# A decoder-layer kernel on one core: edits to the order of five stretches (first loads, a decay row, a state scaling, memory's weights, an output projection)

## The chip, the cores and the metric

The kernel runs on one core of a Trainium2 chip. The time is device microseconds of a whole execution. Before the change three runs took 1079.46, 1080.54 and 1083.1 us; their median is 1080.54. The engines are TensorE (PE; its weight loads are PEld), VectorE (DVE), ScalarE (ACT), GpSimd (POOL) and SyncE (SP, which here only issues loads and stores).

## What is computed

One step of one layer of a hybrid decoder, for a prompt of 512 tokens and 8 samples of 8 tokens, which share the weights (576 columns in all, width 1024). Each part stands between two RMS norms:

```python
proj = rms(x) * g_pre_mix @ w_in                    # z, xbc, dt, q, k, v, gates
y_ssd = ssd_scan(silu(conv(xbc)), dt, a, h_ssm)     # Mamba-2, 16 heads of 64, state 128
y_ssd = rms((y_ssd + d_skip * xs) * silu(z)) * g
h_ml  = rms(mlstm_scan(q, k, v, ig, logf, ...)) * g * sigmoid(og)
x = x + rms(concat(y_ssd, h_ml) @ w_out) * g_post_mix
mk, mv = u_mem @ w_mem_k, u_mem @ w_mem_v           # u_mem = rms(mem) * g_mem
x = x + rms(attention(rms(x) @ w_xq, mk, mv) @ w_xo) * g_post_x
x = x + rms((silu(u @ w_gate) * (u @ w_up)) @ w_down) * g_post_ffn
```

Results are both outputs, the new memory keys and values, and the new SSM, convolution and mLSTM states of both groups.

## The kernel before

Activations lie with the features on the 128 partitions, 8 tiles of 128 by 576 columns, in a handful of large slots (`SL`, numbered) that successive stages take over. The columns are worked in halves of 256 and 320 (288 and 288 from the cross-attention on). The matmuls are in fp32 accuracy by splitting: every operand is a rounded part (`whi`, `uh`, ...) and a rest (`wlo`, `ul`, ...), and each product is three matmuls, L208 (`uh` by `whi`), L209 (`ul` by `whi`) and L211 (`uh` by `wlo`). A weight tile of 128x1024 is therefore loaded by SyncE into `raw` (L181, two buffers), cast by ScalarE into `whi` (L186, three buffers), and subtracted by VectorE into `wlo` (L193); some of the rests come by L190 and L191, ScalarE and an adding load of GpSimd's. PSUM has three pools of banks; `pg`, of three banks, holds the projections' sums, which the other engines empty.

The stages follow one another: a start with warm-up matmuls on zeros (L309, NWARM of them) while the first loads land, the input projection with the scans between its tiles, the output projection (`out1`, `out2`), the memory's keys and values, the cross-attention with its output projection (`xo`), and the FFN. A scheduler sets the order in which each engine's instructions stand, by a model of their times. `tc.issue_after(i)` tells it to place an instruction after `i`; it is an order of placing and adds no wait between engines by itself.

The places that the change touches:

- Start. SyncE first loads `par` (L310, all gains and small parameters, 128x150), then the first pieces of two weight tiles (`raws`, L319 and L322) alternating with pieces of x (`xraw`, L320); two loads stand on ScalarE's queue. `uh` (L332) and `ul` (L333) scale x by a gain out of `par`; VectorE casts the first weights (L329). The first real matmuls are L349 to L351.
- Decay rows, up to 85 us. VectorE computes `sx` (L560, L561) and `gpr` (L563), ScalarE copies both into a row tile `r` (L565, L566), TensorE transposes `r` (`ps_ct`, L587), ScalarE copies the result into `CT` (L589), and the broadcast `ps_en` (L595) reads that. `d1t` (L578) is a rest of another row that VectorE computes for the stacked rows `cumst` and `sxst`.
- Mask products. For each head the SSD scan forms a mask (VectorE L670, ScalarE's exponential L672, the product `lm` with `cbs` L673) which `ps_yi` (L678) multiplies. The products are kept in the list `mults`, eight for each of two groups. Between them GpSimd scales the samples' states by their decay (L789, 128x1024, two for each of four b) after TensorE has read them (`ps_hs`, L781); for b = 2 the source places the scaling after `mults[7]`.
- z, from 245 us. VectorE multiplies z's bank by `rxb` (L1053) to begin its evacuation.
- Memory. `memraw` (slot 1) receives the memory's rows (L1234); four weight tiles of its keys and values go through `raw` like the output projection's own and are split into `wmh` and `wml` (L197, L198). Later slot 1 takes `x` again (L1261, L1262).
- `xo`. Eight tiles; each ends with a square for the norm (L270, L274) and an evacuation into `f_xo` (L1540), both on ScalarE. The first three tiles leave out their last two k until the attention's last head is done.

## Time and profile before

| | |
|---|---|
| median of three runs | 1080.54 us |
| profiled execution | 1079.74 us, span 1078.0 us, granted clock 0.999 |
| loads and stores | 182.02 MB, mean 169 GB/s |
| costliest group of TensorE | L208 of the input projection, 544 matmuls, 161.6 us, 297 ns each |
| costliest group of ScalarE | L186, 104 casts, 105.2 us, 1014 ns each |
| costliest group of VectorE | L193, 96 subtractions, 94.1 us, 982 ns each |

How to read the rows: a row of the timeline has the start and the duration in us, the engine, the line, the operation, output<-inputs with buffer numbers left out, the shapes, and how many instructions of the same kind the row holds; in brackets the idle time of the engine ahead of it and what ended that. An engine name with a q is its queue of load issues. A row of the waits has the waiting instruction, what it waited for, the sum in us, the number of times and the longest. A row of the stretches has the stretch, its length, TensorE's busy time with its number of matmuls, the granted clock as a share of full speed, the share of the load engines in use and GB/s.

### The profile page before, as it was taken

What the parts mean: (1) busy time and instruction counts of PE and PEld (TensorE: products, weight loads), DVE (VectorE), ACT (ScalarE), POOL (GpSimd) and SP (SyncE); (2) the same over time, 40 slices, a digit from 0 to 9 for tenths busy, and PEclk for the clock granted to TensorE, in tenths of its full rate; (3) what the DMA queues carried; (4) which work ended last, traced back from release to release, by engine and by line L of the source; (5) the groups of instructions that cost most, each with busy time, mean ns of one, the idle gap of its engine ahead of it and who ended that gap; (6) DMA issues with size and microseconds to landing.
All of it is one profiled execution on the core that took longest, in us unless ns stands there. A gap on an engine that the chain in (4) does not pass through costs nothing.

```text
span 1078.0 us, 20698 instructions
## 1 busy us (share of the span) xinstructions
PE 1068.0 (99%) x8124; PEld 1014.8 (94%) x8124; DVE 752.0 (70%) x1508; ACT 608.1 (56%) x1094; POOL 231.0 (21%) x304
## 2 busy tenths in 40 slices
PE   9999999999999999999999999999999999999997
PEld 9999887778999999999999989999999999999997
DVE  6897775658877775569755546766467887787556
ACT  7867522345654555556555445645567566656653
POOL 1444643313113121000154301100011111111000
PEclk9999999999999999999999999999999999999999
DMA  6786544426654438753468775743477697578532
GB/s 208 179 168 131 157 126 175 149 71 185 190 154 144 113 113 320 233 205 105 150 202 282 277 253 179 240 131 95 135 165 155 153 203 165 118 186 186 131 132 89
DMA packets 58822, 182.02 MB, mean 169 GB/s; under 512 B 6588, under 2 KB 11836, under 8 KB 58212
## 3 DMA queue, kind: packets, MB, share of 16 engines
q1 hardware_dynamic: 42740, 138.06, 39.2%
q0 software_dynamic: 15408, 41.69, 19.9%
q8 instruction: 64, 1.05, 0.4%
q10 hardware_dynamic: 576, 0.95, 0.3%
q14 instruction: 34, 0.28, 0.1%
HBM read 160.01 MB, written 20.65 MB: 168 GB/s over the span
## 4 chain that ended last, share of the span: by engine, by line
PE 95%; DVE 2%; DMA 2%; ACT 1%; issue 0%; SPq 0%; DVEq 0%; ACTq 0%
PE ps_in L208 6%; PE ps_in L211 6%; PE ps_in L209 6%; PE ps_v L850 5%; PE ps_o L211 3%; PE ps_g L1885 3%; PE ps_u L1885 3%; PE ps_g L1884 3%; PE ps_o L209 3%; PE ps_u L1886 3%; PE ps_g L1886 3%; PE ps_o L208 3%; PE ps_u L1884 3%; PE ps_dn L1884 2%; PE ps_dn L1885 2%; PE ps_dn L208 2%
## 5 line engine op out<-in xcount | busy, mean ns | idle before, releaser
L208 PE MATMUL ps_in<-uh,whi 128*128 128x320 f32 (+1 forms) x544 | 161.6, 297 | 0.3 <-ACT la L448 0.3
L211 PE MATMUL ps_in<-uh,wlo 128*128 128x320 f32 (+1 forms) x544 | 161.6, 298 | 0.0
L209 PE MATMUL ps_in<-ul,whi 128*128 128x320 f32 (+1 forms) x544 | 161.2, 296 | 0.0
L186 ACT CAST whi<-raw 128x1024 fp32r<-128x1024 f32 (+1 forms) x104 | 105.2, 1014 | 98.8 <-PE ps_in L209 25.7
L193 DVE TENSOR_TENSOR wlo<-raw,whi 128x512 fp32r<-128x512 f32 (+1 forms) x96 | 94.1, 982 | 68.7 <-ACT whi L186 67.6
L211 PEld LDWEIGHTS ps_in<-uh,wlo 128*128 128x128 f32 x544 | 102.2, 188 | 1.7 <-issue 1.3
L208 PEld LDWEIGHTS ps_in<-uh,whi 128*128 128x128 f32 x544 | 102.3, 188 | 1.4 <-ACT la L448 0.6
L209 PEld LDWEIGHTS ps_in<-ul,whi 128*128 128x128 f32 x544 | 102.3, 188 | 1.2 <-issue 0.8
L1884 PE MATMUL ps_g<-b,whi 128*128 128x288 f32 x144 | 42.4, 295 | 0.0
L1885 PE MATMUL ps_g<-b,whi 128*128 128x288 f32 x144 | 42.4, 295 | 0.0
L1885 PE MATMUL ps_u<-b,whi 128*128 128x288 f32 x144 | 42.2, 294 | 0.0
L1884 PE MATMUL ps_u<-b,whi 128*128 128x288 f32 x144 | 42.2, 294 | 0.0
L191 POOL DMA_DIRECT2D wlo<-win x31 | 26.9, 866 | 71.1 <-ACT wlo L190 66.6
L198 DVE TENSOR_TENSOR wlo<-sw,whi 128x1024 fp32r<-128x1024 f32 (+1 forms) x26 | 29.6, 1140 | 16.7 <-ACT whi L197 16.6
L1857 ACT CAST whi<-rawx 128x1024 fp32r<-128x1024 f32 (+1 forms) x26 | 25.6, 987 | 26.5 <-PE ps_dn L1885 13.7
L208 PE MATMUL ps_xo<-qh,whi 128*128 128x288 f32 x128 | 38.3, 302 | 0.2 <-ACT whi L186 0.2
L209 PE MATMUL ps_xo<-ql,whi 128*128 128x288 f32 x128 | 37.8, 297 | 0.0
L211 PE MATMUL ps_o<-mixm_h,wlo 128*128 128x256 f32 (+1 forms) x128 | 37.7, 295 | 0.0
L209 PE MATMUL ps_o<-mixm_l,whi 128*128 128x256 f32 (+1 forms) x128 | 37.5, 293 | 0.0
L211 PE MATMUL ps_xq<-u2h,wlo 128*128 128x320 f32 (+1 forms) x128 | 37.5, 294 | 0.0
L209 PE MATMUL ps_xq<-u2l,whi 128*128 128x320 f32 (+1 forms) x128 | 37.4, 294 | 0.0
L211 PE MATMUL ps_o<-mixs_h,wlo 128*128 128x320 f32 (+1 forms) x128 | 37.4, 292 | 0.0
(769 smaller groups left out, 3841.1 us busy)
## 6 DMA issues: line engine op xcount, KB each, us to landing
raw<-win SPq DMA_DIRECT2D x35, 512.0 KB, 4.2
raw<-wout SPq DMA_DIRECT2D x17, 512.0 KB, 3.7
raw<-wxq SPq DMA_DIRECT2D x13, 512.0 KB, 4.3
raw<-wgate SPq DMA_DIRECT2D x13, 512.0 KB, 3.6
raw<-wup SPq DMA_DIRECT2D x13, 512.0 KB, 5.3
wlo<-win POOLq DMA_DIRECT2D x23, 256.0 KB, 5.3
kva<-vc SPq DMA_DIRECT2D x11, 512.0 KB, 6.1
raw<-wv SPq DMA_DIRECT2D x10, 512.0 KB, 4.0
```

The costliest lines, as they stand in the source:

```text
L186: casts.append(A.copy(hi[:, :n], raw[:, :n]))
L191: accs.append(G.dma_start(lo[:, a:b], src[:, a:b], accum_op=ALU.add))
L193: e.tensor_tensor(lo[:, a:b], raw[:, a:b], hi[:, a:b].bitcast(F32), op=ALU.subtract)
L198: (eng or V).tensor_tensor(lo, src, hi.bitcast(F32), op=ALU.subtract)
L208: mm(ps, wh, ah, start=i == 0, stop=False)
L209: mm(ps, wh, al, start=False, stop=False)
L211: m = mm(ps, tiles[order[c]][1], xh(order[c], t0, n), start=False, stop=c == len(tiles) - 1)
L850: mm(ps, a, b, skip_group_check=True, **kw)
L1857: A.copy(s.h3[:, s.all], s.r2[:, s.all])
L1884: mm(ps, wh, b[0][k], start=start and k == 0, stop=False, skip_group_check=True)
L1885: mm(ps, wh, b[1][k], start=False, stop=False, skip_group_check=True)
L1886: m = mm(ps, wl, b[0][k], start=False, stop=k == nk - 1, skip_group_check=True)
```

## The change

Seven edits. (1) NWARM is 17 instead of 21, and `par` is loaded behind the first piece of weights. (2) `d1t` is placed after the second half of `sx`. (3) After the eighth mask product GpSimd copies one column of it into a tile that nothing reads. (4) The evacuation of the first z tile's second half is placed after the last mask product. (5) Memory's slot 1 gets two further places of 1024 columns (`spare`) behind the memory's rows; the four weight tiles are loaded into them in turn instead of into `raw`. (6) The square and evacuation of the first three `xo` tiles are kept back until the fourth tile asks for its weights, and those are asked for after the first tile's end. (7) `evx`, the list of evacuations, keeps its places for that.

```diff
--- before.py
+++ after.py
@@ -107,7 +107,7 @@
 
 CUT = 512
 CCUT = 128
-NWARM = 21
+NWARM = 17
 NSS = 7
 NWX = 3
 TCOPT = dict(schedule_with_timeline_sim=True)
@@ -307,7 +307,6 @@
     psw = MP("ps_warm")
     for _ in range(NWARM):
         mm(psw[:, 0:256], wz[:, 0:128], wz, start=True, stop=True, skip_group_check=True)
-    S.dma_start(par, I["par"])
 
     wl = [wp.tile([P, 1024], F32R, name="wlo", tag="wlo", bufs=3) for _ in range(2)]
     RT = {k: wp.tile([P, 3], F32, name=k + "_r", tag=k + "_r") for k in ("px0", "p30", "px1", "p31")}
@@ -317,6 +316,8 @@
         if k % 2 == 0:
             c = slice(128 * k, 128 * k + 256)
             S.dma_start(raws[0][:, c], I["win"][1][:, c])
+        if k == 0:
+            S.dma_start(par, I["par"])
         xd = (S if k else A).dma_start(xraw[:, k, :], I["xT"][:, k, :])
         if k % 2 == 0:
             xd = (S if k else A).dma_start(raws[1][:, c], I["win"][2][:, c])
@@ -558,7 +559,7 @@
     V.tensor_copy(mp[r4, 512:576].rearrange("p (c t) -> p c t", t=8), m0.unsqueeze(2).to_broadcast([4, 8, 8]))
     sx = row("sx", tag="la")
     V.tensor_tensor(sx[r4, :], cum[r4, :], mrw[r4, :], op=ALU.subtract)
-    V.tensor_tensor(sx[r4, :], sx[r4, :], mp[r4, :], op=ALU.add)
+    sx_done = V.tensor_tensor(sx[r4, :], sx[r4, :], mp[r4, :], op=ALU.add)
     V.tensor_tensor(gpr[r4, :], ig[r4, :], cum[r4, :], op=ALU.subtract)
     V.tensor_tensor(gpr[r4, :], gpr[r4, :], mp[r4, :], op=ALU.subtract)
     r2 = row("r2", 4, tag="i2")
@@ -575,7 +576,8 @@
         G.memset(st_, 0.0)
         V.tensor_copy(bt, src)
         A.copy(st_[0:n, :], bt)
-        V.tensor_tensor(d1, src, bt, op=ALU.subtract)
+        with tc.issue_after(sx_done.ins):
+            V.tensor_tensor(d1, src, bt, op=ALU.subtract)
         V.tensor_copy(bt, d1)
         A.copy(st_[32:32 + n, :], bt)
         V.tensor_tensor(d1, d1, bt, op=ALU.subtract)
@@ -672,6 +674,8 @@
                 exps.append(A.activation(lm, lm, AF.Exp))
                 mults.append(V.tensor_tensor(lm, lm, cbs, op=ALU.mult))
                 lms.append(lm)
+                if len(mults) == 8:
+                    G.tensor_copy(sd.tile([P, 1], F32, name="lm0"), lm[:, 0:1])
 
             for c in range(4):
                 for k in (1, 0):
@@ -1050,7 +1054,8 @@
     def z_evac(j):
         def ev(t0, n, ps):
             t = tmp()[:, 0:n]
-            V.tensor_tensor(ps, ps, rxb[:, t0:t0 + n], op=ALU.mult)
+            with tc.issue_after(mults[15].ins) if t0 and j == 0 else ExitStack():
+                V.tensor_tensor(ps, ps, rxb[:, t0:t0 + n], op=ALU.mult)
             A.activation(t, ps, AF.Tanh, scale=0.5)
             V.scalar_tensor_tensor(t, t, 1.0, ps, op0=ALU.add, op1=ALU.mult)
             yj = y[:, j, t0:t0 + n]
@@ -1220,7 +1225,9 @@
     turns = list(range(len(PRE)))
 
     memh = at.tile([P, 2, KT, 256], F32R, name="memhl")
-    memraw = SL(1, "memraw", F32, (P, KT, 256))
+    mem1 = SL(1, "memraw", F32, (P, 4608))
+    memraw = mem1[:, 0:2048].rearrange("p (k t) -> p k t", t=256)
+    spare = [mem1[:, a:a + 1024] for a in (2048, 3072)]
     rmem_b = at.tile([P, 256], F32, name="rmem_b")
     ssqm, ssq = ssq_tile("ssqm"), ssq_tile("ssqo")
     for j in range(8):
@@ -1269,7 +1276,9 @@
     wm = [(wmh[:, 16 + 1024 * i:1040 + 1024 * i], wml[:, 48 + 1024 * i:1072 + 1024 * i]) for i in range(4)]
 
     def wm_split(i):
-        split_w(I["wmk"][6 + i] if i < 2 else I["wmv"][3][:, i - 2, :], to=wm[i])
+        with tc.issue_after(loads[-1].ins):
+            loads.append(S.dma_start(spare[i % 2], I["wmk"][6 + i] if i < 2 else I["wmv"][3][:, i - 2, :]))
+        split(*wm[i], spare[i % 2])
 
     def chain2(i, js):
 
@@ -1525,10 +1534,17 @@
     evx = []
     ssq = ssq_tile("ssqxo")
 
+    kept_back = []
+
     def xo(j, i, pool=None):
 
         t0, n = EHALVES[i]
 
+        if (j, i) == (3, 0):
+            with tc.issue_after(ends[0].ins):
+                weights(("xo", j), I["wxo"][j], cut=1024)
+            while kept_back:
+                kept_back.pop(0)()
         with tc.issue_after(evx[j - 3].ins if j > 2 else ovs[5].ins):
             ps, w = GP("ps_xo")[:, :n], weights(("xo", j), I["wxo"][j], pool=pool, cut=1024)
 
@@ -1536,9 +1552,18 @@
             m = gemm(ps, [(*w, KT)], act(oh), act(ol), t0, n, k0, k1, [2, 3, 4, 5, 6, 7, 0, 1], 6 if j == 3 else 0)
             if k1 < KT:
                 return m
-            add_sq(ph, ssq, ps, j if i == 0 else XO1.index(j), n, t0=t0)
-            evx.append(A.activation(f[:, j, t0:t0 + n], ps, AF.Copy, scale=PAR("g_postx", j)))
-            return m, evx[-1]
+            at_e = len(evx)
+            evx.append(None)
+
+            def out():
+                add_sq(ph, ssq, ps, j if i == 0 else XO1.index(j), n, t0=t0)
+                evx[at_e] = A.activation(f[:, j, t0:t0 + n], ps, AF.Copy, scale=PAR("g_postx", j))
+
+            if j < 3 and i == 0:
+                kept_back.append(out)
+            else:
+                out()
+            return m, evx[at_e]
         return step
 
     u3_ = SL(3, "u3h", F32R, (P, 5120))
```

How this moves instructions, at three places. GpSimd at 172 us in the profile before, where it scales the states `h` of b = 2 after the first eight mask products; in brackets what each instruction waits for (DMAHW is a load, Pool GpSimd itself). Before:

```order
L789 TENSOR_TENSOR h_1965<-h_1965,vt_1794 128x1024 [waits DMAHW0_49,DMAHW1_49,PE_49,Pool_49]
L789 TENSOR_TENSOR h_1964<-h_1964,vt_1794 128x1024 [waits DMAHW5_49,DMAHW6_49,PE_49,Pool_49]
L693 TENSOR_TENSOR xs<-xs,ec 128x384 [waits DVE_49]
L648 TENSOR_TENSOR xe<-xdt,wend 128x512 [waits DVE_49]
L656 TENSOR_TENSOR hs<-hs,decp 128x512 [waits DVE_49]
```

and now:

```order
L793 TENSOR_TENSOR h_1963<-h_1963,vt_1792 128x1024 [waits DMAHW0_49,DMAHW1_49,PE_49,Pool_49]
L793 TENSOR_TENSOR h_1962<-h_1962,vt_1792 128x1024 [waits DMAHW5_49,DMAHW6_49,PE_49,Pool_49]
L678 COPY lm_1541<-lm 128x1 [waits DVE_49]
L697 TENSOR_TENSOR xs<-xs,ec 128x384 [waits DVE_49]
L650 TENSOR_TENSOR xe<-xdt,wend 128x512 [waits DVE_49]
```

The copy of one column of `lm` stands behind the two scalings, and their own waits are the same as before.

VectorE at 247 us, at the last two mask products (`lm<-lm,cbs`) and the evacuation of z (`ps_in<-ps_in,rxb`). Before:

```order
L670 SCALAR_TENSOR_TENSOR lm<-ps_l,ncum,c_84 128x128 x8
L1053 TENSOR_TENSOR ps_in<-ps_in,rxb 128x320
L673 TENSOR_TENSOR lm<-lm,cbs 128x512 x2
L1053 TENSOR_TENSOR ps_in<-ps_in,rxb 128x256
L193 TENSOR_TENSOR wlo<-raw,whi 128x512
```

and now:

```order
L672 SCALAR_TENSOR_TENSOR lm<-ps_l,ncum,c_84 128x128 x8
L675 TENSOR_TENSOR lm<-lm,cbs 128x512 x2
L1058 TENSOR_TENSOR ps_in<-ps_in,rxb 128x320
L1058 TENSOR_TENSOR ps_in<-ps_in,rxb 128x256
L193 TENSOR_TENSOR wlo<-raw,whi 128x512
```

The evacuation of the 320 columns moved from ahead of the two products to behind them.

ScalarE at 635 us, where the first three `xo` tiles are squared and evacuated and the weights of the next tiles are cast (`whi<-raw`). Before:

```order
L270 ACTIVATE ssqxo_7531<-ps_xo_7541 128x288
L1540 ACTIVATE f_xo_7530<-ps_xo_7541,par_79 128x288
L186 CAST whi_7670<-raw_7668 128x1024
L274 ACTIVATE sq_7605<-ps_xo_7574 128x288
L1540 ACTIVATE f_xo_7530<-ps_xo_7574,par_79 128x288
```

and now:

```order
L186 CAST whi_7653<-raw_7651 128x1024
L270 ACTIVATE ssqxo_7525<-ps_xo_7535 128x288
L1560 ACTIVATE f_xo_7524<-ps_xo_7535,par_79 128x288
L274 ACTIVATE sq_7659<-ps_xo_7566 128x288
L1560 ACTIVATE f_xo_7524<-ps_xo_7566,par_79 128x288
```

The first cast moved from behind the first tile's evacuation to ahead of its square.

## The prediction

> **What bounds the kernel now.** I read the busy table of the page first, then the list of TensorE's waits (what waited, for what, us in all, how often, the longest), then the stretches around them in the order of time.

> ```profile
> span 1078.0 us, 20698 instructions
> ...
> PE 1068.0 (99%) x8124; PEld 1014.8 (94%) x8124; DVE 752.0 (70%) x1508; ACT 608.1 (56%) x1094; POOL 231.0 (21%) x304
> ```

> TensorE is busy for 1068.0 of 1078.0 us, with 1068.0 / 8124 = 0.131 us for a matmul. So only ten microseconds of the span are not matmul time, and whatever the change does to VectorE, ScalarE or GpSimd counts only where TensorE stands still for it. The waits of TensorE name all such places:

> ```profile
> PE ps_yi L678 <- DVE lm L673: 1.1, 1, 1.1
> PE ps_warm L309 <- DVE wz L306: 1.1, 1, 1.1
> PE ps_in L208 <- ACT la L448: 0.3, 1, 0.3
> PE ps_xo L208 <- ACT whi L186: 0.2, 1, 0.2
> ```

> The second row is the program's beginning, which no edit touches. The other three add up to 1.1 + 0.3 + 0.2 = 1.6 us. A matmul's end is modelled in this profile, so a wait can also hide in the overlap of two matmuls; by starts of matmuls I find 0.17 us more at the wait of `ps_xo` and 0.24 us at a mask product at 249 us, both worked out below, and I allow as much for the wait on `la`. The rest of the ten microseconds is the tail after the last matmul, which stays as it is. **The ceiling of this change is therefore about 2 us plus whatever the shorter warm-up gives, 0.2% of the time.** No part shortens a matmul after the start, and none removes one there.

> **The change, part by part.**

> *Start: four warm-up matmuls fewer, parameters behind the first weights.*

> ```profile
> 0.75 0.39 SPq L310 DMA_DIRECT2D par<-par  x1
> 1.20 0.41 SPq L319 DMA_DIRECT2D raw<-win  x1
> ...
> 4.05 0.96 ACT L332 ACTIVATE uh<-xraw,par 128x256 fp32r<-128x256 f32 x2
> 4.77 0.29 DVE L329 CAST whi<-raw 128x256 fp32r<-128x256 f32 x1 [0.68 <-DMA raw<-win]
> 5.38 0.56 PE L349 MATMUL ps_in<-uh,whi 128*128 128x256 f32 x1
> ```

> Today the parameters have landed when the scaling that makes `uh` starts at 4.05, the weights land at 4.77, and the first real matmul issues at 5.38 when the cast (4.77 + 0.29) and the warm-ups are done. Two loads on one queue change places. The weights, issued 0.45 us earlier, should land near 4.77 - 0.45 = 4.3. The parameters, issued where the weights were, land at 4.77 at the latest if they take as long as those, and `uh`, which needs them, starts between 4.05 (nothing lost) and 4.77 (0.7 us lost). The warm-ups:

> ```profile
> 1.30:5.30 4.00, 4.00 (x20) 1.00 0.88 265
> 6.40:7.40 1.00, 1.00 (x10) 1.00 1.04 386
> ```

> Twenty in 4.00 us is one per 0.20 us, against 0.10 from 6.40 on (at mixed widths; 256 columns pass in 0.115 at 249 us), so TensorE works at half pace up to about 6.4 us although the column of the granted clock (the second 1.00) shows no throttling. Four warm-ups fewer release TensorE 4 x 0.20 = 0.8 us earlier, at about 4.6. So the first real matmul issues between 4.7 (all goes well, 0.7 us won) and 5.38 + 0.7 = 6.1 (parameters late). Either end then meets this:

> ```profile
> 33.24 1.05 ACT L186 CAST whi<-raw 128x1024 fp32r<-128x1024 f32 x1 [1.96 <-DVE cb L470]
> ...
> 37.22 0.37 ACT L448 COPY la<-ps_in 40x256 f32<-40x256 f32 x1
> ...
> 37.64 0.39 PE L208 MATMUL ps_in<-uh,whi 128*128 128x256 f32 x1 [0.29 <-ACT la L448]
> ```

> TensorE arrives early at 37.64 and waits for ScalarE to empty a bank. ScalarE's work there, from the cast at 33.24 to the copy that ends at 37.59, hangs on weight loads and on the statistics, not on TensorE's arrival. What TensorE wins at the start it waits here instead; what it loses, up to the 0.29 us shown (0.29 + 0.17 = about 0.45 with a hidden part), the wait swallows. I take **0** for the start; the ends are -0.3 us (if ScalarE moves along) and +0.7 - 0.45, about +0.3.

> [...] The pace in the two rows above agrees with a doubling, at 5.4 us after the first matmul; no row here shows what a pause does.

> *VectorE's `d1t` behind `sx`, before 80 us.*

> ```profile
> 75.54 0.73 DVE L578 TENSOR_TENSOR d1t<-cum,btt 16x576 f32<-16x576 f32 x1
> ...
> 77.96 0.75 DVE L561 TENSOR_TENSOR sx<-sx,mp 4x576 f32<-4x576 f32 x1
> ...
> 78.86 0.67 ACT L566 COPY r<-sx 4x576 f32<-4x576 f32 x1
> ...
> 79.69 0.27 PE L587 MATMUL ps_ct<-c,r 100*128 100x100 f32 x1
> ```

> One operation of 0.73 us leaves VectorE's path to the transposes, so `r` is complete at about 79.53 - 0.7 = 78.8 instead of 79.53. The transposes also stand three matmuls earlier in TensorE's order, 3 x 0.146 = 0.44 us, so they are wanted at 79.25. They did not wait before (no row of the waits names them) and have 0.4 us to spare after: **0**, with +0.3 us as upper end if the copy of `sx` stays at 78.86 behind ScalarE's cast.

> *GpSimd's copy of a mask product.* The largest wait is this one:

> ```profile
> 171.62 0.68 DVE L673 TENSOR_TENSOR lm<-lm,cbs 128x512 f32<-128x512 f32 x1
> ...
> 172.81 2.21 DVE L673 TENSOR_TENSOR lm<-lm,cbs 128x512 f32<-128x512 f32 x1
> ...
> 172.54 4.27 POOL L789 TENSOR_TENSOR h<-h,vt 128x1024 f32<-128x1024 f32 x2 [6.21 <-PE ps_hs L781]
> 177.94 1.01 POOL L693 TENSOR_TENSOR xs<-xs,ec 128x384 f32<-128x384 f32 x1 [1.13 <-DVE ec L691]
> ...
> 175.07 1.09 PE L678 MATMUL ps_yi<-lm,xdt 128*64 128x128 f32 x16 [1.10 <-DVE lm L673]
> ```

> The same mask product takes 0.68 us alone and 2.21 us while GpSimd scales the state, and TensorE waits 1.10 us for it. For this to go, the scalings (L789, started when `ps_hs` is done) would have to wait for the product. The copy reads the product and so waits for it, but on GpSimd's own row it stands **behind** both scalings, as the rows in the section on the change show, and the scalings still wait for TensorE and DMA only. A queue runs in order: what stands behind the scalings cannot hold them. The copy itself lies in the 1.13 us that GpSimd is idle before 177.94 (one column, against 1.01 us for 384), so it costs nothing. **0**; the ends are -1.1 and, if the copy did delay what follows, +0.1.

> [...]

> *VectorE's z evacuation behind the last mask products, 249 us.*

> ```profile
> 247.94 0.63 ACT L672 ACTIVATE lm<-lm 128x512 f32<-128x512 f32 x1 [0.40 <-DVE lm L670]
> ...
> 247.83 0.49 DVE L1053 TENSOR_TENSOR ps_in<-ps_in,rxb 128x320 f32<-128x320 f32 x1
> 248.22 1.28 DVE L673 TENSOR_TENSOR lm<-lm,cbs 128x512 f32<-128x512 f32 x2
> ...
> 249.30 0.28 PE L211 MATMUL ps_in<-uh,wlo 128*128 128x256 f32 x1
> 249.65 0.77 PE L678 MATMUL ps_yi<-lm,xdt 128*64 128x128 f32 x10
> ```

> The products end at 248.22 + 1.28 = 249.50. With the evacuation behind them, the first starts at 247.83, but the second must wait for the exponential, 247.94 + 0.63 = 248.57, and ends at about 248.57 + 0.68 = 249.25. TensorE's earlier matmul allows the next at 249.30 + 0.11 = 249.41, against 249.65: **-0.24 us**. The evacuation now ends near 249.7, with its bank still to be emptied for the next tile; between 0 and -0.24, and I take -0.2.

> *Memory's raw weights in places of their own.*

> ```profile
> 445.65 1.05 ACT L186 CAST whi<-raw 128x1024 fp32r<-128x1024 f32 x1 [0.73 <-DMA raw<-wout]
> ...
> 449.18 0.30 PE L208 MATMUL ps_o<-mixm_h,whi 128*128 128x320 f32 x1
> ...
> 467.10 0.33 SPq L1261 DMA_DIRECT2D x<-xT  x1
> ...
> 491.31 1.28 DVE L1157 TENSOR_TENSOR x<-x,f_mix 128x320 f32<-128x320 f32 x3
> ```

> Four raw loads no longer take turns with the output projection's. TensorE has no wait between 400 and 540 us, so an earlier cast wins nothing. The cast of 445.65 ends 449.18 - 446.70 = 2.5 us before its matmul, so there is room for the few operations that change places. The load of `x` shares the slot of the new places and so waits for the last split; it is issued at 467.10 today and used at 491.31, 24 us later. **0**; the upper end is a rival below.

> *ScalarE's evacuations behind the cast for the fourth `xo` tile.*

> ```profile
> 635.32 0.41 ACT L270 ACTIVATE ssqxo<-ps_xo 128x288 f32<-128x288 f32 x1 [2.99 <-PE ps_xo L211]
> 635.63 0.49 ACT L1540 ACTIVATE f_xo<-ps_xo,par 128x288 f32<-128x288 f32 x1
> 636.01 1.05 ACT L186 CAST whi<-raw 128x1024 fp32r<-128x1024 f32 x1
> 636.95 0.42 ACT L274 ACTIVATE sq<-ps_xo 128x288 f32<-128x288 f32 x1
> ...
> 636.57 0.29 PE L211 MATMUL ps_xo<-qh,wlo 128*128 128x288 f32 x1
> 637.12 0.40 PE L208 MATMUL ps_xo<-qh,whi 128*128 128x288 f32 x1 [0.25 <-ACT whi L186]
> ```

> Today ScalarE runs the square, the evacuation and the cast (635.32 to 637.06), and the matmul at 637.12 takes the cast. After the change the cast comes first, but the fourth tile takes the first tile's bank, so its first matmul now waits for the evacuation instead: the same three operations in another order. What is won is their start. The cast need not wait for the tile's last matmul, only for its weights' buffer, some 0.2 us earlier: 635.1 + 0.94 + 0.31 + 0.49 = 636.84 by the pitches of these rows. TensorE could go on at 636.57 + 0.13 = 636.70, so I take **-0.2 us** (bounds 0 and 637.12 - 636.70 = -0.42).

> **Sum.** 0 + 0 + 0 - 0.2 + 0 - 0.2 = -0.4 us. The profiled execution took 1079.74 us (span 1078.0 and 1.74 around it), so it would be 1079.3. The three runs have a median of 1080.54, 0.8 above the profiled one, so against them I say 1080.1 us. That is 0.04%; a measurement of this kernel can tell about 0.3%, 3.2 us, from no change.

> **Rivals.** *All waits go*: the copy holds the scalings after all (-1.1), both hidden waits close (-0.24 and -0.42) and ScalarE moves along at the start (-0.3): 1080.54 - 2.1 = 1078.5. Against it stands GpSimd's order. *Slower, by the start*: if the pause between the last warm-up (4.6) and a late first matmul restarts the way to full pace, TensorE stays at half pace 5.4 us (the time it took from 1.06 to 6.4) from about 5.6, to 11.0 instead of 6.4: 4.6 / 2 = 2.3 us lost, with 0.7 for the late parameters and less the 0.45 that the wait at 37 us swallows, +2.5 us or 1082.6. It decides when the pause is long enough to count as idle; for it speaks that `uh` now hangs on the later of two loads. *Slower, by the queue*: SyncE issues in order, so if a load into the new places waits for VectorE's split as long as TensorE takes for one weight tile (48 matmuls, 48 x 0.131 = 6.3 us), the output projection's loads behind it come about 6 us late, and past the 2.5 us of room TensorE loses 3.8 us: 1083.9. It decides from a delay of 2.5 us. Against it: today these loads wait for two shared buffers, which is the stricter condition.

> **Chances.** My forecast (within a microsecond of no change) 0.66; all or most waits go 0.14; slower by the start 0.12; slower by the queue, or another new wait of over 3 us, 0.08. Faster by over 0.3% would be more than the ceiling of about 2.5 us, so it would need scatter of the runs (1079.46 to 1083.1) on top: 0.06. Slower by over 0.3% takes the last rival whole and a part of the other: 0.10. The rest, 0.84, is within 0.3%. The range takes in the first two rivals and a microsecond of scatter below: 1077.8 to 1082.8.

> **What would show it.** The wait of `ps_yi` for `lm` stays at about 1.1 us, with one mask product near 2.2 us; the waits for the mask at 249 us and for `whi` at 637 us shrink, the latter naming `f_xo` now; the wait at 37 us takes any value, with the matmul behind it still near 37.6 us. If the mask product at 173 us takes 0.68 us, my reading of GpSimd's order is wrong; if TensorE waits anywhere between 400 and 540 us, that of the memory weights is.

## The result, and the profile after

The changed kernel is slower by a little: a median of 1082.38 us over 22 runs (1079.92 to 1084.19) where the kernel before takes 1080.47 over 22 runs (1079.26 to 1083.94). The ratio is 1.0014 with an interval of 1.0007 to 1.0020, so 0.8 to 2.2 us. That is within the 0.3% that I called no change, but it is clear of the scatter, and I had forecast a gain of 0.4 us.

The profiled execution took 1082.83 us, 3.1 more than that of before. TensorE's busy time is nearly the same (1068.7 against 1068.0 us), so again the waits come first:

```profile
PE ps_in L350 <- ACT uh L333: 1.6, 1, 1.6
PE ps_yi L682 <- DVE lm L675: 1.1, 1, 1.1
PE ps_warm L309 <- DVE wz L306: 1.1, 1, 1.1
PE ps_in L208 <- ACT la L449: 0.7, 1, 0.7
PE ps_os L1444 <- ACT kva L1469: 0.5, 1, 0.5
```

The mask's wait is where it was, with its 1.1 us. The wait at 37 us has become longer, not shorter, although TensorE comes to it later. Two waits are new: one of 1.6 us ahead of the first real matmul, one of 0.5 us in the cross-attention. The wait of `ps_xo` is gone from the list. The start, row by row:

```profile
0.74 0.39 SPq L318 DMA_DIRECT2D raw<-win  x1
...
1.20 0.41 SPq L320 DMA_DIRECT2D par<-par  x1
...
4.76 0.29 DVE L330 CAST whi<-raw 128x256 fp32r<-128x256 f32 x1 [3.76 <-DMA raw<-win]
...
5.42 0.96 ACT L333 ACTIVATE uh<-xraw,par 128x256 fp32r<-128x256 f32 x2 [2.26 <-DMA par<-par]
...
5.98 0.86 PE L350 MATMUL ps_in<-uh,whi 128*128 128x256 f32 x2 [1.58 <-ACT uh L333]
```

The weights, issued 0.46 us earlier, land no earlier: their cast starts at 4.76, where it started at 4.77. The parameters land more than a microsecond later, so that `uh` starts at 5.42 in place of 4.05. The warm-ups end at 4.4, and TensorE stands still for 1.58 us. What comes then is in the stretches behind it (length, TensorE's busy time and matmuls, granted clock, load share, GB/s):

```profile
7.00:8.00 1.00, 1.00 (x6) 0.60 1.06 372
8.00:9.00 1.00, 1.00 (x6) 0.50 0.98 322
9.00:10.00 1.00, 1.00 (x6) 0.50 1.02 327
10.00:11.00 1.00, 1.00 (x8) 0.69 1.03 345
11.00:12.00 1.00, 1.00 (x10) 1.00 1.01 367
```

The granted clock falls to half: the shortfall adds up to (0.40 + 0.50 + 0.50 + 0.31) / 0.50 = 3.4 us at half pace, six matmuls in a microsecond instead of ten, and costs 1.7 us against full pace (the kernel before was itself at half pace up to 6.4 us, so the lag in the table below grows by 1.54 us here). The trace's own record has the fall at 7.21 and the next rise at 10.62 us, 3.41 apart.

How far each place stands behind the same place of before, by the starts of the matmuls in the two timelines:

| place | before | after | behind |
|---|---|---|---|
| first real matmul | 5.38 | 5.98 | 0.60 |
| sums of squares `ps_ss` | 24.38 | 26.52 | 2.14 |
| `ps_in` after the wait for `la` | 37.64 | 40.20 | 2.56 |
| `ps_yi` after the wait for the mask | 175.07 | 177.56 | 2.49 |
| `ps_yi` behind z's evacuation | 249.65 | 252.05 | 2.40 |
| `ps_os`, first of its rows | 603.29 | 606.44 | 3.15 |
| fourth `xo` tile | 637.12 | 640.14 | 3.02 |

So 2.56 of the 3.1 us are lost before 41 us, 0.5 more at the wait of `ps_os`, and little is won. Why the wait at 37 us doesn't swallow the delay is seen on VectorE, which takes the mean of squares from TensorE (the rows of before, then of after):

```profile
24.70 1.23 DVE L193 TENSOR_TENSOR wlo<-raw,whi 128x1024 fp32r<-128x1024 f32 x1 [1.16 <-ACT whi L186]
25.85 0.16 DVE L244 TENSOR_SCALAR rx_v<-ps_ss 128x5 f32<-128x5 f32 x1
```

```profile
25.39 1.23 DVE L193 TENSOR_TENSOR wlo<-raw,whi 128x1024 fp32r<-128x1024 f32 x1 [1.16 <-ACT whi L186]
27.73 0.17 DVE L244 TENSOR_SCALAR rx_v<-ps_ss 128x5 f32<-128x5 f32 x1 [1.11 <-PE ps_ss L234]
```

Before, `rx_v` ran as soon as VectorE was free; after, it waits 1.11 us for TensorE's sums and stands 1.88 us later. VectorE's next subtraction (L193) is behind it in the queue and releases a buffer, SyncE's next weight load waits for that buffer, and ScalarE's cast waits for the load (rows of after):

```profile
29.70 1.28 DVE L193 TENSOR_TENSOR wlo<-raw,whi 128x1024 fp32r<-128x1024 f32 x1
...
31.00 0.33 SPq L181 DMA_DIRECT2D raw<-win  x1
...
35.80 1.05 ACT L186 CAST whi<-raw 128x1024 fp32r<-128x1024 f32 x1 [3.80 <-DMA raw<-win]
...
39.78 0.37 ACT L449 COPY la<-ps_in 40x256 f32<-40x256 f32 x1
```

That cast stood at 33.24 before, 2.56 us earlier, and the copy that TensorE waits for at 37.22, also 2.56 earlier. The delay went once around, through VectorE, a load and ScalarE, and came back to TensorE. It did not come back as the same 2.14 us: the subtraction and the load behind it stand 1.88 to 1.89 us later than before (27.81 for the subtraction there), and this load took 4.7 us to land where its counterpart took 4.0, which adds the other 0.7.

The two small gains are there. At 249 us the products stand in front, and `ps_yi` follows the matmul before it by 0.21 us where it was 0.35; at 637 us the cast stands first:

```profile
251.84 0.28 PE L211 MATMUL ps_in<-uh,wlo 128*128 128x256 f32 x1
252.05 0.44 PE L682 MATMUL ps_yi<-lm,xdt 128*64 128x128 f32 x4
```

```profile
638.34 1.05 ACT L186 CAST whi<-raw 128x1024 fp32r<-128x1024 f32 x1 [2.86 <-PE ps_xo L209]
639.29 0.41 ACT L270 ACTIVATE ssqxo<-ps_xo 128x288 f32<-128x288 f32 x1
639.59 0.49 ACT L1560 ACTIVATE f_xo<-ps_xo,par 128x288 f32<-128x288 f32 x1
...
639.72 0.29 PE L211 MATMUL ps_xo<-qh,wlo 128*128 128x288 f32 x1
640.14 0.40 PE L208 MATMUL ps_xo<-qh,whi 128*128 128x288 f32 x1
```

From `ps_xo`'s last matmul to the next it is now 0.42 us against 0.55 (636.57 to 637.12): 0.13 won. And the copy stands behind the scalings, as GpSimd's rows and VectorE's product show:

```profile
175.02 4.27 POOL L793 TENSOR_TENSOR h<-h,vt 128x1024 f32<-128x1024 f32 x2 [6.21 <-PE ps_hs L785]
179.24 0.18 POOL L678 COPY lm<-lm 128x1 f32<-128x1 f32 x1
```

```profile
175.29 2.21 DVE L675 TENSOR_TENSOR lm<-lm,cbs 128x512 f32<-128x512 f32 x1
```

### The profile page after: what moved, and what is told of

Its sections match the earlier page's. It is cut to its first block, busy times and chain, and to the rows that moved or that the text cites. A ratio compares the mean times of both kernels' runs of the same rounds, so it can differ in the third digit from the quotient of the medians.

```text
span 1081.0 us, 20695 instructions
## 1 busy us (share of the span) xinstructions
PE 1068.7 (99%) x8120; PEld 1015.1 (94%) x8120; DVE 751.9 (70%) x1508; ACT 607.7 (56%) x1094; POOL 231.0 (21%) x305
## 3 DMA queue, kind: packets, MB, share of 16 engines
q8 instruction: 64, 1.05, 0.4%
## 4 chain that ended last, share of the span: by engine, by line
PE 95%; DMA 2%; DVE 1%; ACT 1%; issue 0%; POOL 0%; DVEq 0%; SPq 0%; ACTq 0%
PE ps_in L211 6%; PE ps_in L208 6%; PE ps_in L209 6%; PE ps_v L854 4%; PE ps_o L211 3%; PE ps_g L1910 3%; PE ps_g L1909 3%; PE ps_o L209 3%; PE ps_o L208 3%; PE ps_g L1911 3%; PE ps_u L1910 3%; PE ps_u L1911 3%; PE ps_u L1909 3%; PE ps_dn L1909 2%; PE ps_dn L1910 2%; PE ps_dn L1911 2%
## 5 line engine op out<-in xcount | busy, mean ns | idle before, releaser
L208 PE MATMUL ps_in<-uh,whi 128*128 128x320 f32 (+1 forms) x544 | 161.5, 297 | 0.7 <-ACT la L449 0.7
L211 PE MATMUL ps_in<-uh,wlo 128*128 128x320 f32 (+1 forms) x544 | 161.8, 298 | 0.0
L186 ACT CAST whi<-raw 128x1024 fp32r<-128x1024 f32 (+1 forms) x104 | 105.2, 1013 | 97.9 <-PE ps_in L209 25.6
L193 DVE TENSOR_TENSOR wlo<-raw,whi 128x512 fp32r<-128x512 f32 (+1 forms) x96 | 94.1, 982 | 61.5 <-ACT whi L186 60.6
L211 PEld LDWEIGHTS ps_in<-uh,wlo 128*128 128x128 f32 x544 | 102.2, 188 | 1.9 <-issue 1.3
L208 PEld LDWEIGHTS ps_in<-uh,whi 128*128 128x128 f32 x544 | 102.3, 188 | 1.7 <-ACT la L449 1.0
L208 PE MATMUL ps_xo<-qh,whi 128*128 128x288 f32 x128 | 38.3, 302 | 0.1
L211 PE MATMUL ps_o<-mixm_h,wlo 128*128 128x256 f32 (+1 forms) x128 | 37.7, 295 | 0.0
L211 PE MATMUL ps_xq<-u2h,wlo 128*128 128x320 f32 (+1 forms) x128 | 37.5, 293 | 0.0
L208 PE MATMUL ps_o<-mixm_h,whi 128*128 128x256 f32 (+1 forms) x128 | 37.4, 292 | 0.0
```

The source lines that it names most:

```text
L186: casts.append(A.copy(hi[:, :n], raw[:, :n]))
L193: e.tensor_tensor(lo[:, a:b], raw[:, a:b], hi[:, a:b].bitcast(F32), op=ALU.subtract)
L208: mm(ps, wh, ah, start=i == 0, stop=False)
L211: m = mm(ps, tiles[order[c]][1], xh(order[c], t0, n), start=False, stop=c == len(tiles) - 1)
```

## The experiments

**Theory**: the start makes the whole loss. Late parameters make a pause, the pause takes the clock, and the delay passes through the norm's sums. **Rival**: it comes from further back, the memory's loads and SyncE's order above all. Each ratio is to the kernel before, run beside it on the same chip. The median of that kernel differs by as much as 1 us from one chip's session to another (1080.47 to 1081.47), so ratios are compared. In the expectations, "the first kernel" is e1's and "the second kernel of the first call" is e2's.

*e1: the start put back, all else as changed.*

```diff
-NWARM = 17
+NWARM = 21
+    S.dma_start(par, I["par"])     # ahead of the loop
-        if k == 0:
-            S.dma_start(par, I["par"])
```

> The changed kernel with its start put back (21 warm-ups, parameters loaded ahead of the first weights); the other edits stay. Theory 1, the start makes the loss (late parameters, a pause of TensorE, half clock after it, and the delay passes through the norm's sums to the bank wait near 37 us): the first real matmul issues at 5.4 us again, the granted clock stays 1.00 from 7 to 11 us, the wait for la is about 0.3 us, and the time is 0 to 0.5 us below the kernel before. Theory 2, the loss sits further back (memory's loads and the wait of ps_os near 606 us): still 1 to 1.5 us above the kernel before.

Measured 0.9988 (0.9977 to 0.9998). The first real matmul is at 5.37 again, the clock is full, and the loss is gone. The rest of the change, then, gains 0.2 to 2.5 us. Its profile has a wait that none before had, 0.5 us of `ps_o` for a bank near 447 us:

```profile
PE ps_yi L681 <- DVE lm L674: 1.1, 1, 1.1
PE ps_warm L309 <- DVE wz L306: 1.1, 1, 1.1
PE ps_o L208 <- DVE f_mix L1258: 0.5, 1, 0.5
```

*e5: the start edit alone on the kernel before.*

```diff
-NWARM = 21
+NWARM = 17
-    S.dma_start(par, I["par"])
+        if k == 0:     # in the loop, behind the first raw
+            S.dma_start(par, I["par"])
```

> The kernel before with the start edit alone (17 warm-ups, parameters behind the first weights). Theory 1, the start makes the loss: first real matmul near 6 us, granted clock near 0.5 for about 3.4 us in most executions, a wait for la of 0.3 to 0.7 us, and 2 to 3 us above the kernel before (ratio 1.002 to 1.003). Theory 2, the loss sits in the memory's loads: within 0.5 us of the kernel before.

Measured 1.0013 (1.0002 to 1.0025): in the medians the start alone makes the loss, and e1 shows that without it there is none. The rival falls as the cause of the loss. How the start makes it, this run's profile doesn't show: it had a pause of 1.0 us, yet its clock stayed full, and at the mask's wait it stands only 0.86 us behind the kernel before (175.93 against 175.07). 2.4 us of its time are waits of `ps_o` at 425 and 439 us, where loads landed late, with memory's loads as before. So the 400 to 540 us stretch, which had no wait in the profile I predicted from, has one in other executions with and without the memory edit.

*e4 and e8: the changed kernel with 21 and with 25 warm-ups, parameters still behind.*

```diff
-NWARM = 17
+NWARM = 21     # e8: 25
```

> The changed kernel with 21 warm-ups, parameters still behind the weights. Late parameters make the first real matmul issue at about 6.0 us; the warm-ups end at 5.4, so the pause is 0.6 us in place of 1.6. If the length of the pause decides over the clock, it stays full and TensorE is 0.6 us late, which leaves 0.1 to 0.6 us at the end against the first kernel; if lateness alone decides, the time is that of the changed kernel, 2 us above the first.

> The changed kernel with 25 warm-ups in place of 17, parameters still behind the weights: the warm-ups then last to about 6.1 us and fill most of the pause in front of the first real matmul. If the pause takes the clock: granted clock 1.00 from 7 to 11 us in nearly all executions, TensorE about 0.8 us late, and 0 to 0.7 us below the kernel before. If lateness costs, with or without a pause: 1.5 us above the kernel before, as the changed kernel.

Measured 0.9991 (0.9982 to 1.0000) with 21 and 0.9995 (0.9986 to 1.0004) with 25. The second is the cleanest comparison with the changed kernel, though on another chip: its first real matmul issues at 5.91, as late as the changed kernel's, but the warm-ups last until just before it, and the pace is full from 7 us on:

```profile
7.00:8.00 1.00, 1.00 (x9) 1.00 1.02 374
8.00:9.00 1.00, 1.00 (x10) 1.00 1.03 344
```

The time is 0.19% (2 us) below the changed kernel's. So it is the pause that costs; lateness alone costs little (its `ps_ss` stands at 24.88, 0.5 us behind). In e4's profile the parameters landed later still, the pause was 1.34 us long, and the clock fell to half from 8 to 11 us; its median shows no such loss.

*e3 and e9: parameters in front again, with 17 and with 12 warm-ups.* The pause without the lateness.

```diff
-NWARM = 17
+NWARM = 12     # e3: 17
+    S.dma_start(par, I["par"])     # ahead of the loop, as in e1
```

> The changed kernel with the parameters ahead of the first weights again, but 17 warm-ups. If the late parameters are what costs: the first real matmul issues near 5.1 to 5.4 us, a pause of 0.3 to 0.7 us before it, and the time is within 0.5 us of the first kernel. If the shorter warm-up costs by itself (any pause loses the clock): half clock of about 3.4 us after 7 us, and 1.7 to 2.5 us above the first kernel.

> The changed kernel with the parameters in front again and only 12 warm-ups: these end near 3.6 us and the first real matmul issues on time, near 5.4 us, so that a pause of about 1.7 us stands alone, without lateness. If the pause takes the clock: about 3.4 us at half clock after 7 us in most executions, TensorE 1.7 us late at the norm's sums, and 1 to 1.7 us above the kernel with the start put back. If lateness of the first matmul makes the loss: at that kernel's time, 0.1% below the kernel before.

Measured 0.9996 (0.9985 to 1.0008) with 17 and 1.0006 (0.9996 to 1.0016) with 12, against 0.9988 with 21 (e1). The fewer warm-ups, the longer the pause (none, 0.42, 1.45 us in the profiles) and the slower the kernel, with the first real matmul at 5.25 to 5.4 us throughout. The intervals of neighbours overlap, and those of 21 and 12 still do, by 0.0002. Yet e9's profile showed full clock and `ps_ss` at 24.04. Hence:

*e13, e14 and e15, e16: two more profiled executions each of the changed kernel and of e9's, with no edit.*

> The changed kernel once more, to count how often its pause costs the clock. If the pause is what costs about 2 us in the median: granted clock near 0.50 for 3 to 3.5 us between 6 and 12 us in most looks, and TensorE 2 us late at the norm's sums (ps_ss near 26.5). If it costs seldom: full clock here, ps_ss near 25, and the median's loss is still to be found.

> The changed kernel a third time, for the same count: half clock for 3 to 3.5 us after the pause and ps_ss near 26.5 if the pause costs the clock in most executions, full clock and ps_ss near 25 if it does seldom.

> The kernel with the parameters in front and 12 warm-ups once more. If the pause alone costs the clock in most executions: half clock of 3 to 3.5 us between 6 and 12 us, with the first real matmul on time at 5.2 to 5.4 us. If not: full clock.

> The kernel with 12 warm-ups a third time, for the same count: half clock of 3 to 3.5 us between 6 and 12 us if the pause alone costs it in most executions, full clock if it does seldom.

The changed kernel ran at half pace (five to six matmuls in each microsecond from 7 to 10 us) in both, `ps_ss` at 26.72 and 26.52: with the first profile, in all three. The kernel with 12 warm-ups did in one of its two (`ps_ss` at 26.09, then 24.00): one of three with e9. The same program with the same pause (1.55 and 1.54 us) loses 2.1 us by the norm's sums, or nothing. These are the rows of e15, which lost it:

```profile
7.00:8.00 1.00, 1.00 (x6) 1.00 1.00 323
8.00:9.00 1.00, 1.00 (x6) 1.00 0.99 327
9.00:10.00 1.00, 1.00 (x6) 1.00 1.03 364
10.00:11.00 1.00, 1.00 (x8) 1.00 1.02 372
```

Six matmuls in a microsecond, and the clock's column still says 1.00: it didn't show half pace here, nor for the warm-ups of before. The trace's record of the clock begins with its first rise (at 6.41 us in the kernel before, whose warm-ups from 1.06 us on follow one another at 0.21), and up to there the column reads 1.00. Count the matmuls.

What goes with it is in the same traces, which record when the granted clock steps. In the changed kernel it rises at 3.79 us (the warm-ups go from 0.21 to 0.11 us each), falls at 7.21, rises at 10.62 and falls near the end, at 1075.58; in the kernel before it rises at 6.41 and falls at 1074.78. Counted from the first rise these are 1, 2 and 314 steps, and 313, of one length: (1075.58 - 3.79) / 314 = (1074.78 - 6.41) / 313 = 3.413 us. Worked out from the clock's column, e4's 7.94, 11.36 and 1076.32, e6's 83.04, 86.44 and 1076.32 and e14's 7.24, 10.64 and 1075.60 us stand whole multiples of that length apart, to within 0.02 us. In these five executions the steps lie on a grid, then, and it lies elsewhere from one execution to the next (first rise at 3.79 and at 6.41 us in the two kernels), so the same pause falls into one window of the grid, from one of its places to the next, or across two.

For the other executions of the table I take the same length and count 314 steps back from the fall near the end: 1075.24 us in e15, 1075.80 in e9, 1075.84 in e16, 1076.56 in e5, 1076.72 in e10, 1076.08 in e12, again to about 0.02 us. e13's column shows no fall up to 1078 us; its matmuls pick up between 10 and 11 us, and wherever the grid lies by that, one window holds the whole pause of 1.42 us, which leaves 3.41 - 1.42 = 1.99 us. TensorE's busy time in the window that held all or most of the pause, for the ten executions with a pause of over 1 us near the start:

| execution | window | busy in it | pace behind it |
|---|---|---|---|
| changed kernel, first profile | 3.79 to 7.21 | 1.78 us | half |
| changed kernel, e13 | the 3.41 us around the pause | 1.99 us | half throughout |
| changed kernel, e14 | 3.82 to 7.23 | 1.77 us | half |
| e4 | 4.53 to 7.94 | 2.00 us | half |
| 12 warm-ups, e15 | 3.45 to 6.86 | 1.86 us | half throughout |
| 12 warm-ups, e9 | 4.00 to 7.41 | 2.16 us | full |
| 12 warm-ups, e16 | 4.07 to 7.48 | 2.13 us | full |
| e5 | 4.76 to 8.17 | 2.29 us | full |
| e10 (below) | 4.93 to 8.34 | 2.05 us | full |
| e12 (below), pause across two windows | 4.28 to 7.69, to 11.10 | 2.79, 2.92 us | full |

So there are two ways to lose. The first profile, e14 and e4 had reached full pace and lost it for one window. e13 and e15 had not yet reached it: their last warm-ups are still 0.21 us apart, the window that follows holds the pause, and they stay at half pace up to between 10 and 11 us (six matmuls in the microsecond before, eight in this one, ten in the next). e15's window before the pause held 2.39 us of warm-ups and no rise followed; in the changed kernel's first profile one held 2.73 us, and the rise at 3.79 followed. In these rows 2.00 us or less of work in a window loses and 2.05 us or more keeps; with matmul ends that are modelled, that is an order and not a measured threshold, and no run shows that it is the work in a window which decides.

Not all of e9's loss need be the clock: its profile and e16's, which kept it, wait 1.8 and 1.1 us for `kva` in the cross-attention.

*e10: the first scaling's gains by themselves in front, 17 warm-ups.*

```diff
+    S.dma_start(par[:, 0:8], I["par"][:, 0:8])     # ahead of the loop
         if k == 0:
-            S.dma_start(par, I["par"])
+            S.dma_start(par[:, 8:], I["par"][:, 8:])
```

> The changed kernel, but the eight columns of the parameters that the first scaling needs are loaded by themselves ahead of the first weights, the other 142 columns behind them as in the change; 17 warm-ups. If the late gains are the cause: the scaling starts at about 4 us, the first real matmul issues at about 5.0 us, the pause is under 0.5 us, and the time is 0.5 to 1.5 us below the changed kernel's excess, about that of the kernel before. If the small load is slow itself, the scaling starts as late as in the change and the time stays 1.5 us above the kernel before.

Measured 1.0002 (0.9992 to 1.0011). The first part came as hoped: `uh` starts at 3.85 and the first real matmul issues at 4.83. But x's next piece lands later (its `uh` starts at 7.40, against 5.98 in e1), and TensorE stands still two matmul groups later instead:

```profile
6.23 0.64 PE L353 MATMUL ps_in<-uh,wlo 128*128 128x320 f32 x3
8.23 0.65 PE L351 MATMUL ps_in<-uh,whi 128*128 128x256 f32 x3 [1.36 <-ACT uh L334]
```

The load engines are fully busy in this profile from 6 to 9 us (shares of 1.03, 1.03 and 1.06), so I read the load added in front as what took the time that x's piece lost; no run shows that alone.

*e2, e11 and e7: GpSimd's copy really ahead of the scalings.* On top of e1 (e2), alone on the kernel before, which had no copy (e11), and on e2 with the memory edit undone (e7, the second part of the diff).

```diff
-                    G.tensor_copy(sd.tile([P, 1], F32, name="lm0"), lm[:, 0:1])
+                    held.append(G.tensor_copy(sd.tile([P, 1], F32, name="lm0"), lm[:, 0:1]))
...
-            with tc.issue_after(mults[7].ins) if b == 2 else ExitStack():
+            with tc.issue_after(held[0].ins) if b == 2 else ExitStack():
                 G.tensor_tensor(hn, hn, decs[:, :, bb:bb + 1].to_broadcast([P, 16, 64]), op=ALU.mult)
...
-        with tc.issue_after(loads[-1].ins):
-            loads.append(S.dma_start(spare[i % 2], I["wmk"][6 + i] if i < 2 else I["wmv"][3][:, i - 2, :]))
-        split(*wm[i], spare[i % 2])
+        split_w(I["wmk"][6 + i] if i < 2 else I["wmv"][3][:, i - 2, :], to=wm[i])
```

> As the first kernel of this call, and the two scalings of b = 2 are placed after GpSimd's copy, so that they stand behind it on GpSimd's row and truly wait for the mask product. Theory 1 of this wait, GpSimd's scaling blocks the product: the product takes 0.68 us, the wait of ps_yi for lm goes (-1.1 us) and the time is 1.0 us below the first kernel. Rival: the scalings, 4.3 us long, now end 1 us later and TensorE or VectorE waits for them instead: the gain is under 0.3 us.

> The kernel before with GpSimd's copy ahead of the scalings of b = 2, alone. If the block on the mask product is worth its 1.1 us: the product takes 0.69 us, no wait of ps_yi for lm at 174 us, and 0.7 to 1.1 us below the kernel before (ratio about 0.999). If the later scalings hand it on: within 0.3 us.

> The changed kernel with the start put back, the memory edit undone, and the scalings of b = 2 placed after the copy. If the memory edit costs about 0.5 us and the copy ahead of the scalings wins 0.7: no wait between 400 and 600 us, and about 1079.0 where the kernel before takes 1080.9, the fastest so far. If the memory edit costs nothing it is at the time of the second kernel of the first call, 0.19% below the kernel before.

Measured 0.9981 (0.9971 to 0.9991), 0.9988 (0.9977 to 0.9999) and 0.9976 (0.9967 to 0.9985). In e2's profile the copy is in front, the product takes its 0.69 us, and no wait is left there:

```profile
173.58 0.19 POOL L677 COPY lm<-lm 128x1 f32<-128x1 f32 x1 [7.24 <-DVE lm L674]
173.76 3.84 POOL L792 TENSOR_TENSOR h<-h,vt 128x1024 f32<-128x1024 f32 x2
```

```profile
172.83 0.69 DVE L674 TENSOR_TENSOR lm<-lm,cbs 128x512 f32<-128x512 f32 x1
174.03 0.69 DVE L796 TENSOR_TENSOR h<-h,ps_hu 128x512 f32<-128x512 f32 x1 [0.52 <-PE ps_hu L795]
```

The scalings end 0.8 us later than before (177.60 against 176.81), and nobody waits for them. In e2 and e11 some of the gain is given back at another mask product near 240 us (0.65 and 0.38 us); in e2 ScalarE's exponential stands there behind a cast that waits for a weight load. In e7 there is no such wait. e7 is the fastest of all: 0.24% below the kernel before, with these waits left:

```profile
PE ps_warm L309 <- DVE wz L306: 1.1, 1, 1.1
PE ps_o L208 <- ACT f_mix L1124: 0.2, 1, 0.2
```

*e6: the memory edit alone on the kernel before.*

```diff
+        with tc.issue_after(loads[-1].ins):
+            loads.append(S.dma_start(spare[i % 2], I["wmk"][6 + i] if i < 2 else I["wmv"][3][:, i - 2, :]))
+        split(*wm[i], spare[i % 2])
-        split_w(I["wmk"][6 + i] if i < 2 else I["wmv"][3][:, i - 2, :], to=wm[i])
```

> The kernel before with the memory edit alone. If the wait of ps_o for a bank (0.5 us at 447 us in the run with the start put back) comes from this edit, because VectorE empties the bank behind two splits that it does earlier: the wait is there in this profile too and the time is 0.3 to 1 us above the kernel before. Rival: the wait hangs on when a load lands and is there by chance; time as before.

Measured 0.9990 (0.9981 to 1.0000), so it shows no cost, and no wait stands near 447 us. e2 against e7 (0.9981 with it, 0.9976 without) differs by less than these runs can tell. e6's profile holds the oddest rows of the study, half clock in the middle of the kernel:

```profile
82.00:84.00 2.00, 2.00 (x12) 2.00 (x12) 1.94 (x4) 1.95 (x3) 1.74 (x5) 0.76 0.00 2
84.00:86.00 2.00, 2.00 (x11) 2.00 (x10) 1.94 (x4) 1.99 (x6) 0.00 (x0) 0.50 0.85 264
86.00:88.00 2.00, 2.00 (x13) 1.51 (x12) 1.94 (x6) 1.93 (x4) 0.36 (x2) 0.89 1.05 207
```

*e12: e7 with e10's split loads, 21 warm-ups.*

```diff
-    S.dma_start(par, I["par"])
+    S.dma_start(par[:, 0:8], I["par"][:, 0:8])
+        if k == 0:
+            S.dma_start(par[:, 8:], I["par"][:, 8:])
```

> All that gained: 21 warm-ups, the first scaling's gains ahead of the weights and the other parameters behind them, the scalings of b = 2 behind the copy, d1t behind sx, z's evacuation and the xo evacuations as in the change, memory's loads as before. If the start has nothing more to give (the wait at 37 us takes it): the time of the copy with memory undone, 0.24% below the kernel before. If the earlier start gets through: 0.3 us lower.

Measured 0.9995 (0.9985 to 1.0006), slower than e7, which differs only in the split. In the profiles the pause of 1.1 us behind the first group (as in e10) gives back 0.9 us by the norm's sums (25.42 against 24.52); e12's profile has other waits that e7's hasn't, 0.4 us of `ps_o` and 0.2 us of `ps_ss`, whose tie to the split isn't shown. The version to keep is e7; e2 can't be told from it.

## Why the prediction was wrong, by its own steps

- **Start: sized at 0, with +0.3 as its upper end; it cost 2.56 us in the profile, and the whole change 0.8 to 2.2 us over all runs.** Three of its statements failed. "The parameters ... land at 4.77 at the latest": `uh` started at 5.42, and the weights did not move up at all (4.76). I had taken a load's time to landing as its own and as what it was at the other place: the parameters took 2.9 us in front and 4.1 us behind, the weights 3.6 us behind and 4.0 us in front. Then, I priced the lateness but not the pause: it stood only in the rival "slower, by the start", with the chance of 0.12 and at 1082.6 us. That rival is what happened, and the time lies in the stated range only because the range took it in. Its price (+2.5) was near partly by luck: half pace came for 3.4 us (7.21 to 10.62) rather than the 5.4 I put in, and the wait at 37 us, which was to swallow 0.45 us, swallowed nothing. And "ScalarE's work there ... hangs on weight loads and on the statistics, not on TensorE's arrival" overlooked that the statistics are TensorE's own sums. In the profile before, `rx_v` showed no wait for `ps_ss` only because VectorE was busy for as long. Of the 2.14 us by which the sums were late, 1.88 went on through `rx_v`, and a slower load made it 2.56 at the wait.
- **`d1t` behind `sx`: 0, right**, as far as the traces tell: no wait for `ps_ct` in the changed kernel. e5, e6 and e11, which keep the old order, each wait there 0.2 to 0.3 us, and those with the new order don't. So a small gain is hidden here that the profile of before didn't show.
- **GpSimd's copy: 0, right, and for the reason given.** The copy behind the scalings held nothing: 2.21 us, 1.10 us, the same as before. GpSimd's rows kept the order: the product that the copy reads had ended at 177.50, and the copy started at 179.24, when the scalings were through. e2 and e11 show that the scaling is what held the product (0.69 us in e2 with the copy ahead) and that the wait at 174 us goes with it.
- **z's evacuation: -0.2 forecast, -0.14 measured** (0.35 to 0.21 us between the two matmuls).
- **Memory: 0, right as far as the runs can tell** (e6, e2 against e7). The wait of `ps_os` that is new in the profile is not one of its terms: ScalarE's copy of `kva` stands behind a cast that waits for a weight load, 3.94 us after the change and 2.69 before. It appears in ten of the thirteen profiles with the memory edit (0.2 to 1.8 us) and in one of the five without (e11, 0.7). Whether the edit makes it more frequent was not settled.
- **`xo`: -0.2 forecast, -0.13 measured**, with TensorE waiting for the evacuation as expected.

What stays open: what share of executions loses the clock, and what decides over it. All three profiled ones of the changed kernel lost; with 12 warm-ups and a pause of 1.5 us one of three did. The length of the pause doesn't decide alone: 1.34 us lost in e4, 1.45 us kept in e9, in the order of the busy time left in the window. That time isn't the whole measure either: e6 lost the clock with all but 0.32 us of the 4 us from 78 to 82 counted as busy.

## What to carry to other kernels

An absence of waiting in one profile isn't slack: before a wait is counted on to swallow a delay, follow what it waits for back through every engine, and ask whether the delayed engine feeds it. Warm-up matmuls are there to last until the first real one, so their number and the order of the first loads are one edit, not two; a pause of a microsecond and a half between them cost two microseconds in some executions and nothing in others (12 warm-ups: `ps_ss` at 26.09 in e15, 24.04 in e9). And an instruction meant to hold others in a queue has to stand ahead of them in the built order: there the same copy was worth about a microsecond (e11: 0.1 to 2.5 us), and behind them nothing.
